# Input projection by block products: sums taken from blocks in SBUF, six direct tiles, gates in pieces

## The chip, the cores and the metric

The kernel runs on one core of a Trainium2 chip. The metric is the device time of one execution in microseconds, the median of several runs. The engines are named as the profile names them: PE (TensorE matmul), DVE (VectorE), ACT (ScalarE), POOL (GpSimd) and SP (SyncE, which here only issues loads). POOL issues all stores to DRAM, besides a little arithmetic.

## What is computed

One encoder block over 2048 tokens of width 1024, in float32. Only its first step is touched here: a norm of the input and one combined projection of width 3080, whose columns feed two attentions, a set of forget gates and two sets of values.

```python
h = rmsnorm(x, norm1_g[l])
proj = jnp.einsum('bsd,de->bse', h, w_in[l])
dq, dk, dv, fq, fk, fv, fg = jnp.split(proj, SPLITS, axis=-1)
...
log_f = jax.nn.log_sigmoid((fg + b_f[l]).astype(f32))
cum = jnp.cumsum(log_f, axis=1).transpose(0, 2, 1)
...
x = x + jnp.einsum('bse,ed->bsd', mix, w_out[l])
h2 = rmsnorm(x, norm2_g[l])
...
x = x + jnp.einsum('bsf,fd->bsd', jax.nn.silu(g) * u, w_down[l])
return rmsnorm(x, normf_g)
```

## The kernel before, in words

**Products.** A float32 operand is split into a high part (a cast on ACT, L159) and a low part (a subtraction on DVE, L160), and a product is three matmuls of 128x128 by 128x512: high by high, high by low, low by high. The tokens go in four chunks c of 512 (half 0 is c = 0 and 1, half 1 is c = 2 and 3), the 1024 inputs in two halves kh. So a half has four blocks b11 = (kh 0, first chunk), b21 = (kh 1, first chunk), b12 and b22 (the same of the second chunk), each stored by quarters q of 256 tokens. A pair of weight tiles against a half would be eight block products; the kernel makes seven (P1 to P7, in the order P1, P2, P6, P5, P7, P3, P4) out of sums of blocks of the tokens (P5 = b12 - b11, P7 = b22 - b12, P6 = b22 - P5, P4 = b21 - P6) and sums of blocks of the weights. P1, P2 and P3 take b11, b21 and b22 as they are.

**Stages.** `load_x`, `norm` or `norm_two` and `turn` (transposes on PE into PSUM, L240; gains applied by ACT and DVE, L246 and L248) make a block and store it to DRAM in `hop_d`. At the start the first four weight tiles go *without* sums (`e_major`, L327 to L329, 24 matmuls of 512 columns a chunk), against chunk 0, whose blocks are the operands P1 and P2, and then against chunk 1, whose blocks stand in the places of P4 and P3. During the second of these passes `quarter` loads the stored blocks of half 0 again, in pieces of two of the eight slices, makes the four sums on DVE (L273 to L279), splits P5, P7 and P6 into operands, and stores P4 (`tp_d`). Then a list of steps runs: `Features` (two weight tiles, seven products of 12 matmuls, L429 to L431) for six pairs of tiles, `Values` of half 0 and half 1 (28 steps each), and eight more `Features` for half 1. Ahead of each step stand loads (`advance_loads`), sums of weights (`advance_sums`, L403) and splits (`advance_splits`, 4 steps ahead, 3 in the values). Behind each step `take` copies a sum out of PSUM (L439, on ACT) or adds to it (L441, L444, L447, on DVE). Product P6 is summed into the PSUM bank of P1, and P7 into that of P6, so PE waits for the copy in between. `give` splits the result and stores it through one of three buffers `hl`.

**The background.** From the third step on, one call a step drives a generator `second_half`: load, norm and turn the blocks of chunks 2 and 3, load them again and sum them by `quarter`, then `value_sums` (four times: load the value weights from `w_t`, four sums on DVE, L534 to L541, four stores). What is left of it is run out behind the last of these steps, with `gates(0)`: 32 matmuls (L676 to L679), a copy, a small DMA from partitions 8 to 15 to partitions 0 to 7, sigmoid, log and a scan over time on DVE (L693).

**Order.** The code's own order sets each engine's queue, within which a scheduler may move instructions a little. Buffers are few: `hx` 6 tiles (x rows, blocks, loaded blocks, gates), `rawP` 4 (weights as loaded), `opP` 6 (split weights), `hlP` 3. A load whose buffer is still read waits at the head of SP's queue, and holds what stands behind it.

Of the kernel before, what the change touches and what calls it, by code (L numbers as in the profile page):

```python
# [19 lines left out]
P = 128  # L20
# [39 lines left out]
def block_kernel(  # L60
# [101 lines left out]
    with ExitStack() as c1:  # L162
# [37 lines left out]
        def load_x(t):  # L200
            xt = hxt([P, D], "xt")
            nc.sync.dma_start(out=xt, in_=x[t * P:(t + 1) * P, :])
            return xt

        def norm(xt):
# [3 lines left out]
            for h in range(2):  # L209
                nc.scalar.activation(bank(), xt[:, h * 512:(h + 1) * 512], AF.Square, accum_out=s2[:, h:h + 1])  # L210
            nc.gpsimd.tensor_tensor(ss, s2[:, 0:1], s2[:, 1:2], ALU.add)
            rstd_of(r, ss, 1)
            nc.scalar.activation(xt, xt, AF.Copy, scale=r)

        def norm_two(rows):

            rs = []
            for xt in rows:
# [3 lines left out]
                nc.scalar.activation(bank(), xt[:, 0:512], AF.Square, accum_out=s2[:, 0:1])  # L222
                b = xt[:, 512:1024]
                nc.vector.tensor_tensor_reduce(ut("sq"), b, b, 1.0, 0.0, ALU.mult, ALU.add, s2[:, 1:2])
# [3 lines left out]
            for xt, r in zip(rows, rs):  # L228
                nc.scalar.activation(xt[:, 0:512], xt[:, 0:512], AF.Copy, scale=r)
                nc.vector.tensor_scalar(xt[:, 512:1024], xt[:, 512:1024], r, None, ALU.mult)  # L230

        def turn(c, q, kh, rows, p=None):

            b = hxt([P, 4, 256], "hb")
            for k0 in range(0, 4, 2):
                ps = bank()
                for ki in range(2):
                    for i in range(2):
                        k = kh * 4 + k0 + ki
                        nc.tensor.transpose(ps[:, (2 * ki + i) * P:(2 * ki + i + 1) * P],  # L240
                                            rows[i][:, k * P:(k + 1) * P], ident)
# [12 lines left out]
        def quarter(half, q, k0, early):  # L254

            cs, ks_ = slice(q * 256, (q + 1) * 256), slice(k0, k0 + 2)

            def put(p, src):
                if early and p != "P4":
                    hi, lo = ops_p[p]  # L260
                    split(hi[:, ks_, cs], lo[:, ks_, cs], src)
                else:
                    nc.gpsimd.dma_start(out=tp_d[p][half, k0 // 2, q], in_=src)

            b = {}
            for c in range(2):
                r = hxt([P, 2, 2, 256], "hr")
                for kh in range(2):
# [1464 lines left out]
```

## Time and profile before

| | |
|---|---|
| median of 3 runs | 2878.27 us (2871.42 to 2880.87) |
| the profiled execution, whole | 2875.7 us |
| its span, first to last instruction | 2873.9 us |
| input projection, until PE's last matmul of it | 582.1 us |
| PE busy, and its part of the span | 2757.9 us, 96% |
| DVE, ACT, POOL busy | 1915.9, 1501.2, 635.9 us |
| moved by DMA | 470.77 MB, mean 164 GB/s |

A matmul is pipelined: its row lasts about 0.39 us, and a new one begins every 0.23 us, so PE counts as busy through a row of matmuls and a gap in it is idle time. "PEclk" is the clock granted to PE as a share of 2.4 GHz; at 0.50 it is 1.2 GHz. What ended a gap stands behind an arrow. In the page's 40 slices of the span the first four, to 287 us, show PE at 7 to 8 tenths and the DMA engines at 6 to 8; later PE is at 9 nearly everywhere.

### The profile page before, as it was taken

What the parts mean: (1) busy time and instruction counts of PE and PEld (TensorE: products, weight loads), DVE (VectorE), ACT (ScalarE), POOL (GpSimd) and SP (SyncE); (2) the same over time, 40 slices, a digit from 0 to 9 for tenths busy, and PEclk for the clock granted to TensorE, in tenths of its full rate; (3) what the DMA queues carried; (4) which work ended last, traced back from release to release, by engine and by line L of the source; (5) the groups of instructions that cost most, each with busy time, mean ns of one, the idle gap of its engine ahead of it and who ended that gap; (6) DMA issues with size and microseconds to landing.
All of it is one profiled execution on the core that took longest, in us unless ns stands there. A gap on an engine that the chain in (4) does not pass through costs nothing.

```text
span 2873.9 us, 40778 instructions
## 1 busy us (share of the span) xinstructions
PE 2757.9 (96%) x13938; PEld 2284.1 (79%) x13938; DVE 1915.9 (67%) x3818; ACT 1501.2 (52%) x3004; POOL 635.9 (22%) x1141
## 2 busy tenths in 40 slices
PE   7788999999999999998999999999999999999997
PEld 6666777879999978787877778778888788888886
DVE  6656556678888898887343766665676666665555
ACT  5633544467877878887333433333554433333444
POOL 3343012434344433333111111111000110110001
PEclk9999999999999999999999999999999999999999
DMA  8688644574334223432555544445766333334654
GB/s 289 234 274 272 246 166 159 159 214 142 89 102 122 76 77 102 109 84 81 199 203 185 200 161 155 137 151 191 244 233 225 122 100 102 110 110 145 217 202 161
DMA packets 183760, 470.77 MB, mean 164 GB/s; under 512 B 27968, under 2 KB 44496, under 8 KB 183552
## 3 DMA queue, kind: packets, MB, share of 16 engines
q1 hardware_dynamic: 135264, 324.88, 35.8%
q0 software_dynamic: 48256, 143.28, 14.1%
q8 instruction: 109, 1.79, 0.3%
q14 instruction: 99, 0.81, 0.1%
q10 hardware_dynamic: 32, 0.01, 0.0%
HBM read 316.38 MB, written 151.58 MB: 163 GB/s over the span
## 4 chain that ended last, share of the span: by engine, by line
PE 67%; issue 14%; DMA 4%; POOL 4%; ACT 3%; DVE 2%; SPq 0%; POOLq 0%; DVEq 0%; ACTq 0%
PE ps L1022 6%; PE psF L1359 6%; PE psF L1360 5%; PE psF L1361 5%; PE psF L1479 4%; PE psF L1478 4%; PE psF L1477 4%; PE psS L865 4%; PE psS L866 4%; PE psO L957 3%; PE psO L951 2%; PE psO L950 2%; ACT p_sb L895 2%; PE psF L429 2%; PE psF L430 2%
## 5 line engine op out<-in xcount | busy, mean ns | idle before, releaser
L1359 PE MATMUL psF<-hhP,wop 128*128 128x512 f32 x1232 | 479.2, 394 | 14.1 <-DVE u L1371 8.4
L1360 PE MATMUL psF<-hlP,wop 128*128 128x512 f32 x1232 | 482.0, 391 | 0.0
L1361 PE MATMUL psF<-hhP,wop 128*128 128x512 f32 x1232 | 480.8, 391 | 0.0
L895 ACT ACTIVATE p_sb<-p_sb,mx 128x1024 f32<-128x1024 f32 (+7 forms) x384 | 343.6, 901 | 25.4 <-DVE mx L876 17.5
L1359 PEld LDWEIGHTS psF<-hhP,wop 128*128 128x128 f32 x1232 | 232.3, 189 | 80.3 <-DVE u L1371 19.1
L865 PE MATMUL psS<-ks,q 128*128 128x512 f32 (+2 forms) x640 | 271.3, 424 | 3.6 <-DVE mx L882 2.7
L1361 PEld LDWEIGHTS psF<-hhP,wop 128*128 128x128 f32 x1232 | 232.3, 189 | 49.3 <-issue 0.2
L1360 PEld LDWEIGHTS psF<-hlP,wop 128*128 128x128 f32 x1232 | 232.5, 189 | 45.1
L159 ACT CAST wop<-sP 128x512 fp32r<-128x512 f32 x232 | 143.9, 621 | 235.8 <-PE psF L1361 188.8
L1022 PE MATMUL ps<-ident,p_sb 128*128 128x128 f32 x1632 | 252.2, 275 | 11.6 <-ACT thd L1048 7.5
L1477 PE MATMUL psF<-dop 128*128 128x512 f32 x616 | 239.6, 389 | 0.0
L1478 PE MATMUL psF<-dop 128*128 128x512 f32 x616 | 239.6, 389 | 0.0
L1479 PE MATMUL psF<-dop 128*128 128x512 f32 x616 | 239.6, 389 | 0.0
L866 PE MATMUL psS<-ks,q 128*128 128x512 f32 (+2 forms) x640 | 232.9, 365 | 0.0
L1022 PEld LDWEIGHTS ps<-ident,p_sb 128*128 128x128 f32 x1632 | 195.6, 141 | 43.0 <-ACT thd L1048 9.7
L160 DVE TENSOR_TENSOR wop<-sP,wop 128x512 fp32r<-128x512 f32 x232 | 159.2, 687 | 101.5 <-ACT wop L159 101.0
L159 ACT CAST dop<-wr 128x512 fp32r<-128x512 f32 x154 | 95.8, 622 | 202.9 <-PE psF L1479 187.9
L160 DVE TENSOR_TENSOR dop<-wr,dop 128x512 fp32r<-128x512 f32 x154 | 106.1, 689 | 134.2 <-ACT dop L159 133.9
L1369 ACT COPY u<-psF 128x512 f32<-128x512 f32 x132 | 77.5, 587 | 199.7 <-PE psF L1361 196.9
L429 PE MATMUL psF<-phP,wop 128*128 128x512 f32 x392 | 158.0, 407 | 19.9 <-ACT u L439 12.7
L142 DVE TENSOR_TENSOR th<-ps,th 128x512 fp32r<-128x512 f32 (+1 forms) x232 | 146.9, 650 | 32.5 <-ACT th L141 31.6
L1401 POOL DMA_DIRECT2D a_d<-u x88 | 47.6, 541 | 532.1 <-DVE u L1392 529.4
(257 smaller groups left out, 6434.8 us busy)
## 6 DMA issues: line engine op xcount, KB each, us to landing
ar<-a_d SPq DMA_DIRECT2D x70, 512.0 KB
wr<-in_w_gate_dram SPq DMA_DIRECT2D x44, 512.0 KB, 4.7
wr<-in_w_up_dram SPq DMA_DIRECT2D x44, 512.0 KB, 5.7
a_d<-u POOLq DMA_DIRECT2D x88, 256.0 KB, 3.3
wr<-wd_d SPq DMA_DIRECT2D x40, 512.0 KB, 4.2
we<-in_w_e_dram SPq DMA_DIRECT2D x36, 512.0 KB, 4.6
a_d<-t POOLq DMA_DIRECT2D x66, 256.0 KB, 2.8
q<-fq_d SPq DMA_DIRECT2D x64, 256.0 KB, 4.0
```

The lines of the kernel that those rows point to most:

```text
L159: nc.scalar.copy(hi, src)
L160: nc.vector.tensor_sub(lo, src, f32(hi))
L865: nc.tensor.matmul(pm[:, 0:mw], q[:, m, 0, qc], ks[:, m, cols], start=True, stop=False)
L866: nc.tensor.matmul(pm[:, 0:mw], q[:, m, 1, qc], ks[:, m, cols], start=False, stop=not last)
L895: nc.scalar.activation(pv, pv, AF.Exp, scale=-1.0, bias=st[m], accum_out=acc)
L1022: nc.tensor.transpose(ps[:, (2 * i + s) * P:(2 * i + s + 1) * P], p_of(u, s, m, k0 + i), ident)
L1359: nc.tensor.matmul(acc, o[:, 0, ks_], hh[:, k, :], start=first and k == 0, stop=False, **go)
L1360: nc.tensor.matmul(acc, o[:, 0, ks_], hl[:, k, :], start=False, stop=False, **go)
L1361: nc.tensor.matmul(acc, o[:, 1, ks_], hh[:, k, :], start=False, stop=k == 3, **go)
L1477: nc.tensor.matmul(acc, a[:, 0, bs], w[:, 0, :], start=first and m == 0, stop=False, **go)
L1478: nc.tensor.matmul(acc, a[:, 0, bs], w[:, 1, :], start=False, stop=False, **go)
L1479: nc.tensor.matmul(acc, a[:, 1, bs], w[:, 0, :], start=False, stop=m == NF // 2 - 1, **go)
```

## The change

Six tiles instead of four go without sums against chunks 0 and 1 (`N_DIRECT`), and the list of `Features` of half 0 has five pairs instead of six. `turn` hands back the block it made, which stays in SBUF: for half 0 the blocks of chunk 1 are kept and only those of chunk 0 are loaded again (`load_b`), for half 1 nothing is loaded again. Chunk 1's blocks, and b12 of chunk 3, are not stored any more. `block_sums` takes the place of `quarter`, with whole blocks, in three pieces. The rows of tokens 512 to 767 are loaded into buffers of the sums at once, the other two sets behind them. `norm` scales in two halves. `Features.split("P4")` comes together with P2. `value_sums` sums in place and runs on a generator of its own, every other step from the second on, beside `second_half`, which begins two steps sooner. `gates` writes to one tile, its one DMA and its scan come two steps apart, and they run beside the steps that follow. Splits are 4 steps ahead throughout; the operands of half 1 are asked for at the first step of a product instead of the third, and are split one step later.

```diff
-        tp_d = {p: dram.tile([2, 2, 2, P, 2, 256], F32, name=f"tp_d{p}") for p in ("P5", "P6", "P7", "P4")}
+        tp_d = {p: dram.tile([2, 2, P, 4, 256], F32, name=f"tp_d{p}") for p in ("P5", "P6", "P7", "P4")}
+        N_DIRECT = 6
...
-            nc.scalar.activation(xt, xt, AF.Copy, scale=r)
+            for h in range(2):
+                nc.scalar.activation(xt[h], xt[h], AF.Copy, scale=r)
...
-            nc.gpsimd.dma_start(out=hop_d[c, kh, q], in_=b)
+            if c == 0 or c == 2 or (c, kh) == (3, 1):
+                nc.gpsimd.dma_start(out=hop_d[c, kh, q], in_=b)
...
+            return b
...
-                    nc.sync.dma_start(out=r[:, kh], in_=hop_d[half * 2 + c, kh, q][:, ks_])
-                    b[kh, c] = r[:, kh]
-            b11, b21, b12, b22 = b[0, 0], b[1, 0], b[0, 1], b[1, 1]
-            yield
             nc.vector.tensor_sub(b11, b12, b11)
             nc.vector.tensor_sub(b12, b22, b12)
             put("P5", b11)
+            yield
             put("P7", b12)
+            nc.vector.tensor_sub(b22, b22, b11)
             yield
-            nc.vector.tensor_sub(b22, b22, b11)
             nc.vector.tensor_sub(b21, b21, b22)
             put("P6", b22)
             put("P4", b21)
             yield
...
+            put("P5", a22, a21, a22, ALU.add)
+            put("P7", a21, a11, a21, ALU.subtract)
             yield
...
+            put("P6", a11, a22, a11, ALU.subtract)
+            put("P3", a12, a12, a11, ALU.subtract)
             yield
...
-        first = [Features(0, e) for e in (4, 6, 10, 12, 14, 8)]
+        first = [Features(0, e) for e in (6, 10, 12, 14, 8)]
...
-                s[1].split(*s[2:])
+                if s[0] == "val":
+                    s[1].split(*s[2:])
+                elif s[2] != "P4":
+                    s[1].split(s[2])
+                    if s[2] == "P2":
+                        s[1].split("P4")
...
+            if e in (0, 2):
+                q = e // 2
+                pieces = block_sums(0, q, *b0, *hb[q])
+            next(pieces, None)
+            if e % 2:
+                next(pieces, None)
+            if e == 1:
+                b0 = load_b(0, 1)
...
-                g, g2 = ut("g"), ut("g2")
-                nc.scalar.copy(g[0:16, :], ps[0:16, :])
-                nc.sync.dma_start(out=g2[0:8, :], in_=g[8:16, :])
-                nc.vector.tensor_add(z[0:8, j, :], g[0:8, :], g2[0:8, :])
+                nc.scalar.copy(z[0:16, j, :], ps[0:16, :])
+                yield
+            g = hxt([P, 2, 512], "gl")
+            nc.sync.dma_start(out=g[0:8], in_=z[8:16])
+            yield
+            yield
+            nc.vector.tensor_add(z[0:8], z[0:8], g[0:8])
...
-            advance_splits(at + (3 if val else 4))
+            advance_splits(at + 4)
             s[1].multiply(*s[2:])
+            if gate:
+                next(gate, None)
...
-                    elif at > 2:
-                        next(bg, None)
+                    if at > 0:
+                        next(bg[0], None)
+                    if at % 2:
+                        next(bg[1], None)
...
-                if v.half == 0 and s[3] == 2:
+                if v.half == 0 and s[3] == 0:
                     waiting.append(load_op(1, s[2]))
-                if s[3] == 0 and (v.half == 0 and m or v.half == 1 and m == 0):
+                if s[3] == 1 and (v.half == 0 and m or v.half == 1 and m == 0):
```

Three places in the queues. First PE, at the turn of the last rows of chunk 1 (16 transposes), before, where `phP_148` is the operand P4 that holds chunk 1's first block:

```order
L329 MATMUL psF<-phP_138,wop 128x512
L240 MATMUL psF<-ident,xt 128x128 x16
L327 MATMUL psF<-phP_148,wop 128x512 x3
L328 MATMUL psF<-plP_149,wop 128x512
L329 MATMUL psF<-phP_148,wop 128x512
```

and now, where `phP_136` is the operand P1, chunk 0's:

```order
L334 MATMUL psF<-phP_138,wop 128x512
L246 MATMUL psF<-ident,xt 128x128 x16
L332 MATMUL psF<-phP_136,wop 128x512
L333 MATMUL psF<-plP_137,wop 128x512
L334 MATMUL psF<-phP_136,wop 128x512
```

Between the turn and the first product with the block that it makes there now stand the 24 matmuls of the sixth tile against chunk 0. Second, SP's queue while half 1's blocks are made, from a late set of rows (`xt`) on, before (`hr<-hp_d` loads blocks again, `wv<-in_w_t` loads value weights, for sums at L530):

```order
L202 DMA xt<-in_x_dram 128x1024 x2
L269 DMA hr<-hp_d 128x512 x8
L306 DMA we<-in_w_e_dram 128x1024 x2
L530 DMA wv<-in_w_t_dram 128x512 x2
L269 DMA hr<-hp_d 128x512 x6
L369 DMA cossin<-in_rope_dram 128x1x512 x2
```

and now, around the last set of rows (L535 is the old L530; L477 loads value weights for products):

```order
L311 DMA we<-in_w_e_dram 128x1024 x2
L535 DMA wv<-in_w_t_dram 128x512 x3
L209 DMA xt<-in_x_dram 128x1024 x2
L535 DMA wv<-in_w_t_dram 128x512
L477 DMA wv<-in_w_t_dram 128x2x512 x4
L374 DMA cossin<-in_rope_dram 128x1x512 x2
```

The loads of blocks are gone, and the loads for the value sums stand between those of the weights and those of x. Third, POOL's queue around the first norm of chunk 2 (`ss`, `rstd`), before:

```order
L356 DMA fq_d_86<-hl 256x1x256 x2
L211 TENSOR_TENSOR ss<-s_1004 128x1
L137 TENSOR_SCALAR rstd<-ss 128x1
L138 TENSOR_TENSOR rstd<-rstd,mhalf 128x1
L211 TENSOR_TENSOR ss<-s_1040 128x1
```

and now:

```order
L340 DMA fk_d_89<-hl 128x512
L542 DMA wv_d<-wv 128x512
L218 TENSOR_TENSOR ss<-s_1097 128x1
L542 DMA wv_d<-wv 128x512
L137 TENSOR_SCALAR rstd<-ss 128x1
L218 TENSOR_TENSOR ss<-s_1134 128x1
L138 TENSOR_TENSOR rstd<-rstd,mhalf 128x1
```

The norm's three small instructions now stand among the stores of the first value sums, which wait for DVE.

## Rows read from the trace of the kernel before

**Rows 1.** Busy time by stage: us, busy of PE, PEld, DVE, ACT, POOL, PEclk, DMA share, GB/s.
```profile
0.00:45.00 45.00, 32.15 (x188) 29.18 (x189) 29.68 (x65) 30.16 (x59) 19.44 (x43) 1.00 0.78 278
45.00:300.00 255.00, 210.19 (x875) 164.74 (x874) 162.67 (x260) 116.38 (x213) 90.72 (x162) 0.90 0.79 270
300.00:582.00 282.00, 278.88 (x1221) 224.30 (x1220) 164.02 (x242) 122.59 (x201) 68.17 (x119) 1.00 0.54 177
```

**Rows 2.** Waits of PE from 45 to 300 us: in total, times, the longest.
```profile
PE psF L429 <- ACT u L439: 10.9, 2, 7.2
PE psF L240 <- ACT xt L213: 10.6, 5, 4.9
PE psF L431 <- DVE wop L160: 6.4, 1, 6.4
PE psF L489 <- DVE wop L160: 6.1, 2, 4.1
PE psF L429 <- DVE u L441: 5.2, 2, 4.1
PE psF L327 <- ACT phP L159: 4.9, 1, 4.9
PE psF L429 <- ACT wop L159: 0.6, 1, 0.6
```

**Rows 3.** Busy time in the eight stretches at half clock before 300 us.
```profile
279.64:283.05 3.41, 3.41 (x10) 2.64 (x9) 2.29 (x4) 2.42 (x5) 0.00 (x0) 0.50 1.01 390
...
sum 51.20, PE 34.90 PEld 27.32 DVE 32.51 ACT 21.01 POOL 13.40; mean PE 4.36 PEld 3.41 DVE 4.06 ACT 2.63 POOL 1.68
```

**Rows 4.** Busy time in a full stretch, and the two with most DMA.
```profile
150.00:175.00 25.00, 23.66 (x103) 18.70 (x101) 17.14 (x29) 11.30 (x24) 16.87 (x31) 1.00 0.92 313
275.00:300.00 25.00, 18.91 (x68) 14.68 (x68) 17.38 (x26) 12.09 (x20) 2.70 (x5) 0.86 0.95 351
300.00:350.00 50.00, 50.00 (x222) 41.20 (x221) 30.21 (x40) 26.07 (x40) 6.47 (x12) 1.00 0.70 245
```

**Rows 5.** Timeline at 53 us: start, length, what [idle before, what ended it].
```profile
52.07 1.99 ACT L159 CAST phP<-hb 128x1024 fp32r<-128x1024 f32 x2 [2.90 <-DVE hb L246]
53.17 1.22 PE L327 MATMUL psF<-phP,wop 128*128 128x512 f32 x2 [4.86 <-ACT phP L159]
```

**Rows 6.** Timeline of DVE before PE's wait that ends at 86.1 us.
```profile
76.00 0.69 DVE L273 TENSOR_TENSOR hr<-hr 128x512 f32<-128x512 f32 x1 [1.53 <-DMA hr<-hp_d]
85.36 0.68 DVE L160 TENSOR_TENSOR wop<-we,wop 128x512 fp32r<-128x512 f32 x1
```

**Rows 7.** Timeline of a norm and the turn behind it, 132 to 142 us.
```profile
132.09 0.60 ACT L210 ACTIVATE psF<-xt 128x512 f32<-128x512 f32 x1 [3.35 <-DMA xt<-in_x_dram]
139.34 1.01 POOL L138 TENSOR_TENSOR rstd<-rstd,mhalf 128x1 f32<-128x1 f32 x1
141.59 1.75 PE L240 MATMUL psF<-ident,xt 128*128 128x128 f32 x7 [4.94 <-ACT xt L213]
```

**Rows 8.** Timeline of SP and DVE before PE's wait that ends at 207.2 us.
```profile
197.39 2.25 SPq L269 DMA_DIRECT2D hr<-hp_d  x2
203.47 0.69 DVE L274 TENSOR_TENSOR hr<-hr 128x512 f32<-128x512 f32 x1 [8.01 <-DMA tp_dP<-hr]
```

**Rows 9.** Timeline of SP and ACT before PE's waits at 236 and 242 us.
```profile
204.79 21.56 SPq L530 DMA_DIRECT2D wv<-in_w_t_dram  x6
234.29 1.14 ACT L159 CAST wop<-wv 128x512 fp32r<-128x512 f32 x2 [7.77 <-DMA wv<-in_w_t_dram]
```

**Rows 10.** Timeline of DVE and ACT before PE's waits at 279 and 293 us.
```profile
273.16 2.28 DVE L693 TENSOR_TENSOR_SCAN ge<-gone,gz 8x1024 f32<-8x1024 f32 x1
291.19 0.62 ACT L159 CAST fvo<-uv 128x512 fp32r<-128x512 f32 x1 [4.40 <-DMA fv_d<-fvo]
```

**Rows 11.** DMA issues from 0 to 300 us: count, KB each, median us to landing.
```profile
xt<-in_x_dram SPq DMA_DIRECT2D x16, 512.0 KB, 5.7
...
tp_dP<-hr POOLq DMA_DIRECT2D x20, 256.0 KB, 5.1
...
hr<-tp_dP SPq DMA_DIRECT2D x16, 256.0 KB, 6.9
```

More of the change, by code (lines that the diff above doesn't have):

```diff
@@ L198, in hlt, with load_x @@
             return hlp.tile(shape, dt, name=name, tag="hl")
-        def load_x(t):
+        def load_x(t, parts=False):
+            if parts:
+                xt = [sumP.tile([P, 512], F32, name="xh", tag="s") for _ in range(2)]
+                for h in range(2):
+                    nc.sync.dma_start(out=xt[h], in_=x[t * P:(t + 1) * P, h * 512:(h + 1) * 512])
+                return xt
             xt = hxt([P, D], "xt")
             nc.sync.dma_start(out=xt, in_=x[t * P:(t + 1) * P, :])
-            return xt
+            return [xt[:, 0:512], xt[:, 512:1024]]
         def norm(xt):
@@ L282, in quarter, with load_b @@
             yield
+        def load_b(c, q):
+            r = [hxt([P, 4, 256], "hr") for _ in range(2)]
+            for kh in range(2):
+                nc.sync.dma_start(out=r[kh], in_=hop_d[c, kh, q])
+            return r
         def load_op(half, p):
@@ L288, in load_op @@
                 if p in tp_d:
-                    for k in range(2):
-                        nc.sync.dma_start(out=r[q][:, 2 * k:2 * k + 2], in_=tp_d[p][half, k, q])
+                    nc.sync.dma_start(out=r[q], in_=tp_d[p][half, q])
                 else:
@@ L709, in second_half @@
             yield
-            ahead = []
+            yield
+            b = []
             for n, (c, q) in enumerate(todo_):
-                rows, nxt = nxt, None
+                rows = nxt
                 for r in rows:
@@ L715, in second_half @@
                     yield
+                yield
                 for kh in range(2):
-                    turn(c, q, kh, rows)
+                    b.append(turn(c, q, kh, rows))
                     yield
@@ L720, in second_half, with all_sums @@
                     nxt = load(n + 1)
-                for a in ahead:
-                    yield from a
-                ahead = []
                 if c == 3:
-                    ahead = [quarter(1, q, k0, False) for k0 in (0, 2)]
-            for a in ahead:
-                yield from a
+                    yield from block_sums(1, q, *b)
+                    b = []
+        def all_sums():
             for k in range(4):
                 yield from value_sums(k)
-        bg = second_half()
+        bg = [second_half(), all_sums()]
         waiting = []
+        gate = None
         for at, s in enumerate(steps):
@@ L745, in block_kernel @@
                         put_op(*waiting.pop(0))
-                    elif at > 2:
-                        next(bg, None)
+                    if at > 0:
+                        next(bg[0], None)
+                    if at % 2:
+                        next(bg[1], None)
                     if at == n_first - 1:
-                        for _ in bg:
-                            pass
-                        gates(0)
+                        for g in bg:
+                            for _ in g:
+                                pass
+                        gate = gates(0)
+                        next(gate)
+                        next(gate)
             else:
@@ L756, in block_kernel @@
                 v, m = s[1], ORDER.index(s[2])
-                if v.half == 0 and s[3] == 2:
+                if v.half == 0 and s[3] == 0:
                     waiting.append(load_op(1, s[2]))
-                if s[3] == 0 and (v.half == 0 and m or v.half == 1 and m == 0):
+                if s[3] == 1 and (v.half == 0 and m or v.half == 1 and m == 0):
                     put_op(*waiting.pop(0))
                 if v.half == 1 and s[2] == "P4" and s[3] == 3:
-                    gates(1)
+                    gate = gates(1)
+                    next(gate)
+                    next(gate)
+        for _ in gate:
+            pass
     with ExitStack() as c2:
```

86 lines of the change are left out of this document (38 added, 48 removed).

## The prediction

> **What bounds the kernel now.** I read the busy time by stage first. From 300 us on PE is full (278.9 of 282 us) at full clock; from 45 to 300 us it is busy 210.2 of 255 us, at a mean clock of 0.90 [rows 1]. From the last `Features` on, the instructions of all queues stand as they did, so all that the change can give lies before 582 us, and nearly all of it between 45 and 300. I read PE's waits there next: seven groups, together 10.9 + 10.6 + 6.4 + 6.1 + 5.2 + 4.9 + 0.6 = 44.7 us [rows 2]. Then the clock: behind the waits it stands at 0.50 (1.2 GHz) in eight stretches, in which PE works 34.9 us [rows 3]; at full clock that is half, so they cost 17.4 us. What can be won is 44.7 + 17.4 = 62.1 us, 2.2% of the execution. No engine but PE is full in this stage (DVE 162.7, ACT 116.4, POOL 90.7 of 255 us); the DMA engines are the nearest, at 0.79 and 270 GB/s [rows 1]. So PE waits not for work that is too much but for work that comes late in a queue, and the question is which of these waits the new order removes and which it makes.
>
> **The waits that go.** *The turn of the passes, 4.9.* PE's first product with chunk 1 stands right behind the transposes that make its last quarter, and waits for eviction and cast [rows 5]. Now 24 matmuls of the sixth tile stand between. A matmul costs 50 / 222 = 0.225 us in a full stretch [rows 4], so the cover is 5.4 us against a wait of 4.9. It just holds; were the cover gone, the 4.9 would be back.
>
> *The start of the features, 6.4 + 0.6 and one of 1.1 behind it.* DVE has the last quarter's sums and splits in its queue, which waited for a loaded block at 76.0, and comes to the weights' split at 85.4 [rows 6]. The new pass has six tiles, 6 x 24 x 0.225 = 32 us instead of 22, for the same sums, and half of the blocks need no load. I take all of it.
>
> *The norms of chunks 2 and 3, 10.6 in five waits.* ACT stands 3.4 us for rows of x, POOL's power comes late, and PE waits 4.9 [rows 2, 7]. The change puts one more step (12 x 0.225 = 2.7 us) between norm and turn. What is left of it, I put into the next part.
>
> *Half 1's blocks, 7.2.* DVE stands 8.0 us in a sum whose operand SP asked for at 197.4, 2.3 us of issuing and a landing before it [rows 8]; ACT's copy of P6 waits behind it. The arrow names a store, but that instruction reads only loaded blocks. Now the blocks are in SBUF and the load is gone. All of it.
>
> *The end of the features, 3.7 + 4.1.* SP spends 21.6 us on six loads for value sums, because their buffers are taken, and the first value weights behind them keep ACT 7.8 us [rows 9]. Now these sums come in earlier steps and the first value weights are asked for while features run. All of it.
>
> *The first values, 6.1 in two waits.* The gates' scan, 2.3 us, stands before splits on DVE, and a store of `fvo` keeps ACT 4.4 us [rows 10]. The scan moves on by steps and splits are one step (2.7 us) further ahead. The store stays slow, so between 2.0 (the first wait alone) and 6.1 go; I take 6.1, since the second wait, 4.1, has 2.7 us more cover and its casts come in front of the last `fvo`.
>
> With the waits goes the half clock behind them.
>
> **What is added.** *Matmuls.* Two more tiles without sums are 2 x 2 x 24 = 96 matmuls, a pair by products is 7 x 12 = 84: 12 more, 12 x 0.225 = 2.7 us on PE. DVE loses four sums and three additions and gains one split, ACT three copies for one cast; both have room, so that counts nothing.
>
> *The first turns.* ACT's queue now has two Squares of the next rows ahead of the cast of P2's second quarter; 2 x 0.60 = 1.2 us [rows 7]. If it hides, 0; if the whole chain of the norm comes in front, a wait like the longest for a norm, 4.9 [rows 2]. I take 1.2, since PE has another tile's matmuls to do.
>
> *The feature stretch.* Here the change adds waits. SP waits for P4's second half to be stored before it may load it: 5.1 + 6.9 = 12.0 us from the last sum [rows 11], and behind it stand x of chunk 2 and the first value weights; ACT's cast of P4 stands ahead of the copy of P1 that PE needs for P6. POOL has four stores of value sums around the first norm's instructions, and they wait for DVE, which waits for the value weights. A weight buffer comes free only when a value sum's store has landed. I don't price each one, since they share one resource, and bound the stretch by its transfers. From the first rows of chunk 2 to the last product of the features it moves, in units of 512 KB: x 8, value weights for sums 8, weights 6, first value weights 6, rotation tables 2, P4 1; stored 22 of results, 6 of blocks, 8 of sums, 8 of value sums; 75 in all, 39.3 MB. PE's work in it is 5 x 84 x 0.225 = 94.5 us and 64 transposes at 0.125 (1.75 / 7 at half clock [rows 7], halved), 102.5 us. At the fastest 25 us of the trace, 351 GB/s, the transfers take 112 us, at the next, 313, they take 126, at the stage's mean of 270 they take 146 [rows 1, 4]. I take the mean of the two fast ones, 332: 118 us, 16 over PE's work, since the stretch holds more bytes in a microsecond of PE's work (0.38 MB) than either of the two carried. The bounds are 0 (stores trail into the values, where the share falls) and 43.
>
> The Trainium skill has a rule that speaks against the change here: "DMA: Bandwidth & Descriptors", section Specifications, gives about 358 GB/s as a core's part of the memory's bandwidth. By it the 39.3 MB would take 110 us, an estimate, and the forecast would be about 9 us lower than by my 332. The trace agrees over 25 us, where 351 is the most, and not over 3.4 us, where 390 GB/s went through [rows 3].
>
> *The rest.* Gates beside the values, operands of half 1 asked for earlier, norms in two halves: POOL, ACT and DVE do the same work in smaller pieces while PE is full, so they count nothing. Without that cover it would be the scan, 2.3 us [rows 10].
>
> **The sum.** The profiled execution took 2875.7 us, 2.6 below the median of the runs. 2875.7 - 44.7 - 17.4 + 2.7 + 1.2 + 16 = 2833.5; with 2.6 for the median, 2836.
>
> **The rivals.**
> *A, the transfers set the pace.* The stretch gets no faster a rate than the stage's mean, and costs 43 instead of 16: 2836 + 27 = 2863. For it speaks that 50 us at 0.9 of the DMA engines are already there [rows 4]; against it, that less is moved than before (no blocks loaded again for half 1).
> *B, nothing new waits.* Stores trail, the norms are in time: 2836 - 16 - 1.2 = 2819. For it: value weights are asked for four steps, 10.8 us, ahead of their sums, and x's landing takes 5.7 [rows 11]. Against: the rows of chunk 3 are still normed in the call that loads them.
> *C, slower.* Each of the eight background loads (four sets of x, four of value weights) stops ACT or DVE in its queue until it lands, as the load did that ends at 203.5 [rows 8], and PE loses 7.2 us with it and an eighth of today's clock loss, 2.2. That is 8 x 9.4 = 75 in place of 16: 2836 + 59 = 2895. It decides from (62.1 - 3.9) / 8 = 7.3 us a load on; up to there the change still wins. For it: SP's queue has these loads in front of x. Against it: the two sets of chunk 2 and all value weights are asked for two to four steps (5.4 to 10.8 us) ahead of use.
> *D, no change.* The waits move and keep their sum, because PE was only waiting for the slowest queue in another place: 2870 to 2887.
>
> **How the numbers follow.** Forecast 0.50, with 2824 to 2852 as its own range (the stretch between 4 and 32); A 0.22, B 0.12, C 0.08, D 0.08. The range takes the forecast, B and most of A: 2819 to 2868. A measurement of this kernel tells 0.3%, 8.6 us, from no change. Faster by more than that: 0.50 + 0.22 + 0.12 less a little of A's upper end, 0.83; within it 0.09; slower 0.08.
>
> **What would show it.** Right: no wait of PE behind the last transposes of chunk 1; no wait for DVE's splits at the first feature; PE's last matmul of the projection at about 540 us instead of 582; waits of PE in the stage of 10 to 20 us in all, nearly all for norms and for the copy of P1; DMA share of the feature stretch near 0.9. A shows as that share with waits of PE spread over all products; B as a stage without waits above 2 us; C as waits of ACT and DVE for x and value weights of 7 us and more, eight times. Wrong would be the whole reading if the stage's waits go and the end does not come sooner, or if attention or the feed-forward part, which have the same instructions, changed by more than some us.

## The result and the profile after

| | before | changed |
|---|---|---|
| median of 4 runs | 2877.07 us (2871.42 to 2880.87) | 2841.62 us (2838.60 to 2842.74) |
| span of the profiled execution | 2873.9 us | 2840.9 us |
| PE's last matmul of the projection begins | 582.1 us | 549.5 us |

The ratio is 0.9877, 95% interval 0.9858 to 0.9895: 1.2% faster. The forecast was 2836, with 2819 to 2868 as its range, so it was 5.6 us too low. The end of the projection, forecast at about 540 us, came at 549.5. All of the gain lies in the projection: it ends 32.6 us sooner, the span is 33.0 us shorter. What comes behind has the same instructions and took 2291.8 and 2291.4 us.

The busy time by stage of the changed kernel, with the columns of [rows 1]:

```profile
0.00:45.00 45.00, 29.88 (x181) 26.70 (x182) 29.36 (x65) 29.75 (x59) 18.41 (x41) 0.96 0.75 271
45.00:300.00 255.00, 241.58 (x1057) 193.91 (x1055) 179.69 (x261) 135.22 (x240) 87.22 (x154) 0.96 0.80 273
300.00:550.00 250.00, 245.66 (x1060) 196.10 (x1058) 141.17 (x211) 104.78 (x175) 64.71 (x113) 0.99 0.51 164
```

From 45 to 300 us PE is now busy for 241.6 us where it was for 210.2 [rows 1]: 13.4 us idle instead of 44.8. PE's waits in that stretch, against the seven groups of [rows 2]:

```profile
PE psF L434 <- ACT u L444: 9.6, 3, 4.0
PE psF L246 <- ACT xt L221: 3.7, 3, 1.9
```

Of the old groups only the transposes' wait for a norm is still there, with 3.7 us for 10.6. There is none at the turn of the passes, at the first feature, at the sum of half 1's blocks, at the end of the features or at the first values. What is left beside it are three waits of P6 for ACT's copy of P1. The clock did not follow. The stretches of the stage at half clock, with PE's busy time in each, to be held against [rows 3]:

```profile
110.12:113.53 3.41, 3.41 (x10) 0.50 0.91 353
130.60:134.01 3.41, 3.41 (x10) 0.50 0.87 283
157.90:161.31 3.41, 3.21 (x8) 0.50 0.60 183
164.73:168.14 3.41, 3.33 (x14) 0.50 1.01 334
181.80:188.63 6.83, 5.32 (x13) 0.50 0.78 229
sum 20.47, PE 18.68; mean PE 3.74
```

PE still works 18.7 us at 1.2 GHz, where it worked 34.9. Waits fell to 30%, the half clock to 54%.

The three waits for the copy end at 129.5 (3.04), 158.1 (2.55) and 183.3 us (4.03), and each has another cause. Here is the first, on ACT: the norm's two scalings stand in the queue ahead of the copy (L444) and wait for POOL's power.

```profile
125.58 0.60 ACT L159 CAST hl<-u 128x512 fp32r<-128x512 f32 x1
127.64 1.33 ACT L221 ACTIVATE xt<-xt,rstd 128x512 f32<-128x512 f32 x2 [1.45 <-POOL rstd L138]
128.87 0.56 ACT L444 COPY u<-psF 128x512 f32<-128x512 f32 x1
```

The second, on POOL and DVE: P6 of half 1 is summed in place, over block b22, and so waits until the store of that block (L256) has landed, 8.8 us after its issue. Behind the sum stands the addition for the feature's result, and ACT's cast of that result stands ahead of the copy.

```profile
145.67 0.59 POOL L256 DMA_DIRECT2D hp_d<-hb  x1
154.48 1.23 DVE L277 TENSOR_TENSOR hb<-hb 128x1024 f32<-128x1024 f32 x1 [3.49 <-DMA hp_d<-hb]
```

The third, on SP and ACT: the last rows of x are asked for at 171.4, and ACT's squares wait 5.98 us for them with the copy behind. On SP they stand right behind three loads of value weights (L535), and the first of these has waited 7.8 us for the store of a value sum to land and free its buffer (the first line, from SP's waits between 90 and 240 us: in total, times, the longest). So the value sums beside the features make this wait; e8 bears it out.

```profile
SPq L535 <- DMA wv_d<-wv: 11.0, 2, 7.8
169.93 1.46 SPq L535 DMA_DIRECT2D wv<-in_w_t_dram  x3
171.43 1.00 SPq L209 DMA_DIRECT2D xt<-in_x_dram  x2
179.47 0.60 ACT L217 ACTIVATE psF<-xt 128x512 f32<-128x512 f32 x1 [5.98 <-DMA xt<-in_x_dram]
```

### The profile page after: what moved, and what is told of

The parts are those of the page before. It is cut to its first block, busy times and chain, and to the rows that moved or that the text cites. A ratio compares the mean times of both kernels' runs of the same rounds, so it can differ in the third digit from the quotient of the medians.

```text
span 2840.9 us, 40678 instructions
## 1 busy us (share of the span) xinstructions
PE 2753.1 (97%) x13950; PEld 2282.7 (80%) x13950; DVE 1910.0 (67%) x3788; ACT 1502.0 (53%) x3004; POOL 629.8 (22%) x1125
## 3 DMA queue, kind: packets, MB, share of 16 engines
q0 software_dynamic: 47232, 140.14, 13.8%
## 4 chain that ended last, share of the span: by engine, by line
PE 67%; issue 18%; POOL 4%; DMA 4%; ACT 4%; DVE 3%; SPq 0%; POOLq 0%; DVEq 0%; ACTq 0%
PE ps L1056 6%; PE psF L1393 6%; PE psF L1394 6%; PE psF L1395 6%; PE psF L1513 4%; PE psF L1512 4%; PE psF L1511 4%; PE psS L899 4%; PE psS L900 4%; PE psO L991 3%; PE psO L985 2%; PE psO L984 2%; PE psF L434 2%; PE psF L436 2%; PE psF L435 2%
## 5 line engine op out<-in xcount | busy, mean ns | idle before, releaser
L1393 PE MATMUL psF<-hhP,wop 128*128 128x512 f32 x1232 | 478.4, 394 | 13.4 <-DVE u L1405 10.9
L1394 PEld LDWEIGHTS psF<-hlP,wop 128*128 128x128 f32 x1232 | 231.8, 188 | 44.8
L434 PE MATMUL psF<-phP,wop 128*128 128x512 f32 x364 | 147.3, 409 | 13.5 <-ACT u L444 10.5
```

The lines of the kernel that those rows point to most:

```text
L1393: nc.tensor.matmul(acc, o[:, 0, ks_], hh[:, k, :], start=first and k == 0, stop=False, **go)
L1394: nc.tensor.matmul(acc, o[:, 0, ks_], hl[:, k, :], start=False, stop=False, **go)
```

## The experiments

Two theories of what makes the time of the feature stretch. **Queues**: each new wait comes from an instruction that stands in the wrong place of one queue, and bytes don't matter. **Transfers**: the stretch lasts as long as its 39 MB take, as the prediction had it for its term of 16 us. Beside them the question whether half clock follows the waits.

All times in one table. The ratio is to executions of the kernel before that were taken beside the kernel in its row, so it can order two rows otherwise than the medians. "End" is the start of PE's last matmul of the projection, "idle" is 255 us less PE's busy time from 45 to 300, "half" is PE's busy time there at half clock, each from one profile. What follows the projection has the same instructions in all of them and took from 2282.7 to 2294.7 us in the profiles, so the end tells an edit apart better than the time does.

One profile says less about "half" than about the rest, since the half clock varies without any edit. Behind the projection the same instructions work from 15.8 to 33.3 us at half clock in the fourteen profiles (idle 51.9 to 59.8 us). At 17 to 21 us, before any of the edits e1 to e12 takes hold, it is 3.0 to 3.4 us in four of the thirteen changed kernels and nothing in nine. So I also give the mean granted clock of whole executions where a fall of "half" is read as a gain: it was 0.986 to 0.989 in the four of the changed kernel, and 0.001 of it stands for 5.7 us at half clock.

| kernel | median, us | ratio to before, 95% interval | end | idle | half |
|---|---|---|---|---|---|
| before | 2877.1 | 1 | 582.1 | 44.8 | 34.9 |
| changed | 2841.6 | 0.9877 (0.9858 to 0.9895) | 549.5 | 13.4 | 18.7 |
| e1 norm in two steps | 2834.7 | 0.9859 (0.9843 to 0.9876) | 543.8 | 13.1 | 6.6 |
| e2 more steps | 2842.2 | 0.9881 (0.9861 to 0.9901) | 546.8 | 16.3 | 11.1 |
| e3 P2 twice | 2832.0 | 0.9850 (0.9833 to 0.9868) | 543.2 | 7.3 | 3.4 |
| e4 more bytes, early | 2841.5 | 0.9878 (0.9857 to 0.9900) | 550.2 | 17.8 | 15.3 |
| e5 more bytes, in the features | 2844.5 | 0.9884 (0.9853 to 0.9916) | 553.4 | 23.4 | 14.0 |
| e6 mended | 2836.7 | 0.9861 (0.9833 to 0.9889) | 542.3 | 13.7 | 6.8 |
| e7 four tiles without sums | 2849.5 | 0.9908 (0.9884 to 0.9932) | 553.5 | 20.7 | 18.5 |
| e8 value sums late | 2841.5 | 0.9877 (0.9852 to 0.9902) | 555.9 | 23.5 | 13.8 |
| e9 P1 ahead | 2840.8 | 0.9887 (0.9866 to 0.9908) | 544.9 | 13.4 | 14.7 |
| e10 all mends | 2832.3 | 0.9854 (0.9834 to 0.9873) | 534.2 | 10.4 | 8.7 |
| e11 blocks loaded again | 2850.4 | 0.9916 (0.9895 to 0.9936) | 565.7 | 29.1 | 22.4 |
| e12 gates at once | 2839.0 | 0.9877 (0.9860 to 0.9893) | 545.3 | 13.9 | 12.5 |

### Do the transfers set the pace? (e4, e5)

```diff
+                    if at % 2 == 0:
+                        nc.gpsimd.dma_start(out=more_d[at // 2], in_=f32(ops_p["P1"][0][:, 0:2, :]))
```

> At every second step of the first five features POOL stores another 512 KB, a piece of operand P1, to a scratch tensor: 18 stores, 9.4 MB more in the stretch. Transfer theory, as the prediction had it: 9.4 MB at 332 GB/s, 28 us more. Queue theory: 18 issues of 0.55 us on POOL and landings somewhat longer, 0 to 8 us more.

This run missed its place. The scheduler issued the 18 stores as soon as their operand was there, from 27.8 to 66.1 us, ahead of the features, so the run says nothing on the features. It shows something else. The row of 45 to 93.5 us, the passes without sums:

```profile
45.00:93.50 48.50, 48.50 (x224) 40.39 (x223) 37.81 (x50) 23.89 (x38) 15.47 (x26) 1.00 0.98 377
```

For 48.5 us 377 GB/s went through, at a DMA share of 0.98, and PE waited for nothing. In e5 the same stores are held in their places on POOL's queue (`tc.keep_in_program_order`); they go out from 95.6 us on.

> As the run with more bytes, but the 18 extra stores of 512 KB are held in their places on POOL's queue, so that they go out during the first five features (there they had all gone out between 28 and 66 us, before the features). Transfer theory, as the prediction had it: 9.4 MB at 332 GB/s, 28 us more. Queue theory: 18 issues of 0.6 us on POOL, landings longer by some us, so that two or three waits of 2 to 5 us grow or come: 2 to 12 us more.

The time rose by 2.9 us and the end of the projection by 3.9, not by 28. From the first to the last product of the features, the changed kernel first, then e5:

```profile
93.45:221.64 128.19, 114.77 (x490) 91.60 (x489) 80.47 (x129) 63.82 (x133) 55.91 (x100) 0.92 0.83 281
```

```profile
93.00:228.90 135.90, 112.48 (x490) 89.96 (x489) 80.95 (x129) 64.20 (x133) 63.35 (x117) 0.91 0.91 321
```

The stretch grew by 7.7 us and moved 321 GB/s in place of 281. So in the changed kernel the transfers had room left, and they do not set its pace. Seventeen of the 18 stores fall into it. Bytes do cost something: idle time rose from 13.4 to 23.4 us, one wait of 8.9 us for a norm among it, in whose chain ACT stands 5.9 and 2.7 us for rows of x. Transfer theory falls in the form in which the prediction used it.

### The waits one by one (e1, e2, e6)

```diff
-                for r in rows:
-                    norm(r)
-                    yield
+                r0 = squares(rows[0])
+                yield
+                scale(rows[0], r0)
+                r1 = squares(rows[1])
+                yield
+                scale(rows[1], r1)
                 yield
```

> In the background of the features a norm is written in two steps: its squares in one, its scaling in the next one, behind the copies of the step between. Queue theory: the wait of 3.0 us at 129.5 us (PE for ACT's copy of P1, which stands behind a scaling that waits 1.45 us for POOL's power and takes 1.3 us itself) goes, and its stretch of half clock with it, 1.7 us; the other two waits for that copy have other causes and stay. Projection ends at 545 to 547 us instead of 549.9, the time falls by 3 to 5 us; the transposes may wait 1 to 2 us more, since scaling comes later. Transfer theory (the stretch lasts as long as its 39 MB): the wait shows up elsewhere, the end stays within 1 us.

The wait of 3.0 us is gone. ACT in e1, at the place that answers to 127 us above (L447 is the copy): no scaling stands between.

```profile
127.08 0.58 ACT L221 ACTIVATE psF<-xt 128x512 f32<-128x512 f32 x1
127.61 0.19 ACT L221 ACTIVATION_READ_ACCUMULATOR psF<-xt 128x1 f32 x1
127.70 0.56 ACT L447 COPY u<-psF 128x512 f32<-128x512 f32 x1
```

But the idle time as a whole is what it was, 13.1 for 13.4 us: the transposes, whose rows are now scaled a step later, wait 7.8 instead of 3.7. PE's waits in e1:

```profile
PE psF L249 <- ACT xt L214: 7.8, 5, 3.4
PE psF L437 <- ACT u L447: 3.5, 3, 2.4
PE psF L437 <- DVE u L449: 1.7, 2, 0.9
```

The projection ends 5.7 us sooner all the same, and in the stage that is the clock: half-clock work fell from 18.7 to 6.6 us, which is 6.0 us of time. The other executions bear it out: the mean granted clock was 0.990 to 0.993 in the four of e1, and each of them is shorter than each of the changed kernel's. That the clock follows from the edit is likely by this; why it does, with the same idle time, is not shown.

```diff
+                if c == 3:
+                    yield
+                    yield
                 for r in rows:
...
                 if c == 3:
+                    yield
                     yield from block_sums(1, q, *b)
```

> Two empty steps between the load of chunk 3's rows and their norm, one empty step between the last turn of a quarter and its sums, both times. Queue theory: the wait of 2.5 us at 158.1 us (DVE's sum in place stands 3.5 us for the store of the block it overwrites) and that of 4.0 us at 183.3 us (ACT's squares stand 6.0 us for rows of x) go, with 1.7 and 2.7 us of half clock: 11 us in all at most, 6 to 11 less time, projection ends at 539 to 544. The sums of the last quarter come five steps (13 us) later, which the first values may feel by up to 3 us. Transfer theory: no change beyond 1 us.

A miss. The squares no longer wait for x, but ACT's copy at 184.1 is as late as before, now behind a scaling. And the empty step ahead of the sums did not keep them apart from the turn. On POOL and DVE of e2:

```profile
200.63 0.59 POOL L270 DMA_DIRECT2D tp_dP<-hb  x1 [6.79 <-DVE hb L272]
203.44 0.55 POOL L256 DMA_DIRECT2D hp_d<-hb  x1 [2.22 <-DVE hb L252]
212.27 1.22 DVE L277 TENSOR_TENSOR hb<-hb 128x1024 f32<-128x1024 f32 x1 [6.72 <-DMA hp_d<-hb]
```

The scheduler had moved P5's sum (L272) in among the evictions of the turn, so the order in the code is not the order in the queue, and the sum over b22 (L277) stands close behind the block's last eviction (L252). POOL stands idle until that eviction and then issues the store of b22 (L256) at once; the store of P5 (L270) in front of it costs nothing there. The store lands 8.7 us after its issue, and the sum waits 6.7 of them; PE then waits 5.4 us at 214. So this wait is the landing itself, and the edit put no distance between the store and the sum.

e6 has e1's edit, holds P5's store behind the store of b22 (`tc.issue_after`), puts the squares of chunk 1's rows behind the casts of P2 at the start, and gives the gates two more steps before their scan.

> Four edits at once, each against one wait of the changed kernel: a norm's scaling one step behind its squares (as in the first experiment), the store of P5 behind the store of the block that the next sum overwrites (it stood in front, and DVE's sum waited 3.5 and 5.1 us for the late landing), the gates' scan two steps later in half 1, and at the start the squares of the next rows behind the casts of P2. Queue theory with the clock on the waits: PE's idle time between 45 and 300 us falls from 13.4 to 5 to 8 us, its half-clock work from 18.7 to under 7, the 3.0 us at 408 us go with their 2.9; the time falls to 2824 to 2831. If something shared is behind the waits: they move, and it stays at 2834 to 2842.

Queue theory expected 5 to 8 us of idle time, and 13.7 were measured. The long waits are gone but for one of 2.6 us, and ten of 0.4 to 1.9 stand in their place. The wait at 402 us stayed (3.1). And the new order of the stores did not shorten DVE's waits for the landing: 5.0 and 3.7 us in the two sums over b22, where the changed kernel has 3.5 and 5.1.

```profile
147.75 1.23 DVE L286 TENSOR_TENSOR hb<-hb 128x1024 f32<-128x1024 f32 x1 [4.99 <-DMA hp_d<-hb]
201.15 1.22 DVE L286 TENSOR_TENSOR hb<-hb 128x1024 f32<-128x1024 f32 x1 [3.73 <-DMA hp_d<-hb]
```

In the stage only the clock paid: 6.8 us of half-clock work (mean granted clock of the four executions 0.989 to 0.990). So the edits moved the waits, as the rival said, and yet the projection ended 7.2 us sooner.

### More cover (e3, e9, e10)

```diff
+            again = s[1].op.get("P2") if at in (8, 15, 22) else None
             s[1].multiply(*s[2:])
+            if again:
+                s[1].multiply("P2", again)
```

> In the three features in which PE waits for the copy of P1, the twelve matmuls of P2 are issued twice, the second time over the first: 36 matmuls more, 8.1 us of work, in front of those waits. If the half clock hangs on the waits: 9.6 us of waits and 6.0 us of clock go against 8.1 us of work, so the time falls by 4 to 7.5 us though PE does more. If half clock comes from something else in the stretch: between 1.5 us less and 0.5 more. If transfers set the pace: no change.

The second product goes into the same bank, over the first. With 36 matmuls more the projection ends 6.3 us sooner than in the changed kernel. By the medians the kernel is 9.6 us faster; in the profiles, too, some 6 us more come from behind the projection, where the instructions are the same. PE's waits in e3:

```profile
PE psF L246 <- ACT xt L221: 4.8, 4, 1.9
PE psF L434 <- ACT u L444: 1.7, 2, 1.1
PE psF L434 <- DVE u L446: 0.8, 1, 0.8
```

The waits for the copy fell from 9.6 to 1.7 us, half-clock work in the stage from 18.7 to 3.4. In the stage that is 6.1 us of waits and 7.7 of clock against 8.1 us of work: 5.7. The waits alone would not pay for the work; the clock does, and it stood higher in all four executions (0.991 to 0.992). It bears out that clock is lost with the waits and that filling them with work, even useless work, can give it back. e9 tries the same cover without work: the first product of a feature goes ahead of the last one of the feature before, so that 24 matmuls stand between P1 and P6.

```diff
+        for n in range(7, n_first, 7):
+            steps[n - 1], steps[n] = steps[n], steps[n - 1]
```

> In the first five features the P1 of a feature is issued ahead of the P4 of the one before, so that two products (24 matmuls, 5.4 us) instead of one stand between P1 and the P6 that needs its copy; no work is added. If those waits come from a cover that is too short, as the run with P2 twice suggests (waits of the stage 13.4 to 7.3 us): waits fall by 5 to 9 us, half-clock work by 8 to 14 (4 to 7 us of time), 2827 to 2833. If the gain there came from the longer stretch of PE's work, which gave all other queues 8 us more: the waits move to the transposes and the end, 2836 to 2842.

The waits for the copy halve, those for the norm more than double, and the idle time is 13.4 us again:

```profile
PE psF L246 <- ACT xt L221: 8.7, 3, 3.4
PE psF L434 <- ACT u L444: 4.8, 2, 4.2
```

So the cover of one product is not the cause by itself, and the time lies in the range of the second reading. What e3 gave and e9 does not are 8.1 us more of PE's work in the stretch, in which all queues get on. That this is the cause is argued, not shown. e10 joins e6 and e9, adds one step before the transposes, and holds the gates' last DVE instructions back.

> The mended kernel with P1 ahead as well, one empty step more between the last scaling and the transposes, and the gates' last DVE work held in its place in the queue. Cover theory: the waits at P6 and before the transposes are both gone but for 2 to 5 us, the 3.1 us at 402 us go, half-clock work in the stage under 4 us: 2820 to 2828. Against it: as in the mended kernel the waits that are removed come back at other places, 2832 to 2838.

```profile
PE psF L443 <- DVE u L455: 8.2, 4, 3.4
PE psF L443 <- ACT u L453: 1.9, 2, 1.2
PE psF L445 <- DVE wop L160: 0.2, 1, 0.2
```

The time lies in the range against cover theory, which had 2820 to 2828. Waits for norms are gone. What is left stands behind the sums in place on DVE and its splits. The wait at 408 us is gone too: PE idles 0.9 us from 300 us on, where the changed kernel idles 4.3. The projection ends at 534.2, 15.3 us sooner. By the medians the gain is 9.3 us, less than in the profiles (13.1). e3 and e10 are both faster than before. Each of their executions is shorter than each of the changed kernel's, though the intervals of the ratios overlap; between the two no difference can be told.

### Parts of the change undone (e7, e8, e11, e12)

```diff
-        N_DIRECT = 6
+        N_DIRECT = 4
...
-            if e in (2, 4):
-                q = e // 2 - 1
+            if e in (2, 3):
+                q = e - 2
...
-        first = [Features(0, e) for e in (6, 10, 12, 14, 8)]
+        first = [Features(0, e) for e in (4, 6, 10, 12, 14, 8)]
```

> Four tiles without sums instead of six, six features instead of five, the rest as changed. By the prediction's steps the waits at the turn of the passes (4.9) and at the start of the features (8.1) come back with their half clock (up to 8), less 12 matmuls (2.7): 10 to 18 us more than the changed kernel, 2852 to 2860. Rival: the kept blocks alone, and splits asked for earlier, remove those waits: 2839 to 2846.

7.9 us slower, between the two theories. The turn of the passes waits again, the start of the features does not: its first product (L434) follows the last direct one without a gap.

```profile
53.43 0.50 PE L332 MATMUL psF<-phP,wop 128*128 128x512 f32 x1 [3.80 <-ACT phP L159]
...
77.40 0.39 PE L334 MATMUL psF<-phP,wop 128*128 128x512 f32 x1
77.62 0.39 PE L434 MATMUL psF<-phP,wop 128*128 128x512 f32 x1
```

```diff
-                    if at % 2:
-                        next(bg[1], None)
```

> The value sums are not run beside the features any more but all behind the last of them. By the prediction's steps the waits at the end of the features come back (7.8 us and 5.1 us of half clock), while the waits behind POOL's value-sum stores (1.8 us at 108 us, 1.9 at 164, part of the 3.0 at 129) go: 4 to 11 us more than the changed kernel, 2846 to 2853. Rival: moving them into the features only moved the waits: 2838 to 2844.

A wait behind the features is there again, now at the first values, and longer than the two it stands for (7.8):

```profile
249.38 0.79 PE L493 MATMUL psF<-wop,phP 128*128 128x512 f32 x1 [13.36 <-ACT wop L159]
```

The features, though, took 118.9 us instead of 127.8, with 10.1 us idle. Without the value sums' loads in front of them, the rows of x keep ACT 1.7 us where they kept it 9.0 (ACT's waits from 95 to 222 us, the changed kernel first, then e8), and of PE's waits for the copy one of 1.6 us is left.

```profile
ACT psF L217 <- DMA xt<-in_x_dram: 9.0, 2, 6.0
```

```profile
ACT psF L217 <- DMA xt<-in_x_dram: 1.7, 1, 1.7
```

So the value sums beside the features cost them 8.9 us, 3.3 of it idle time and 5.4 half clock, and save a longer wait behind them: by the end of the projection the changed order wins 6.4 us. The time itself shows no difference (2841.5): what follows the projection took 2282.7 us in this profile, the least of all, with the least idle time of all there (51.9 us) and 20.1 us at half clock where the changed kernel has 33.3.

```diff
-            if c == 0 or c == 2 or (c, kh) == (3, 1):
+            if c != 1:
...
                 if c == 3:
+                    b = load_b(2, q) + load_b(3, q)
+                    yield
                     yield from block_sums(1, q, *b)
```

> The blocks of half 1 are stored and loaded again for their sums, a step before them, as in the kernel before; all else as changed. By the prediction's step the 7.2 us wait behind the sum that stands for a loaded block comes back, with 2 to 3 us of half clock, less the wait of 2.6 us for the in-place sum (the loaded copy has no store to wait for): 4 to 8 us more than the changed kernel, 2846 to 2850. Rival: one step and the landing of 6.9 us are covered by the spare steps: 2839 to 2844.

8.8 us slower, a little above what was expected; the projection ends 16.2 us later. DVE's first sum stands for the loaded blocks:

```profile
160.40 1.23 DVE L272 TENSOR_TENSOR hr<-hr 128x1024 f32<-128x1024 f32 x1 [9.97 <-DMA hr<-hp_d]
```

PE waits 7.84 us at 164.1 and 9.15 at 231.6 behind such sums.

```diff
                         gate = gates(0)
-                        next(gate)
-                        next(gate)
+                        for _ in gate:
+                            pass
...
                     gate = gates(1)
-                    next(gate)
-                    next(gate)
+                    for _ in gate:
+                        pass
```

> The gates of both halves are written in one go again, behind the last feature of half 0 and the last values of half 1, in place of pieces beside the steps that follow; splits stay four steps ahead. By the prediction's step the waits at the first values come back, the scan's 2.0 us and perhaps the 4.1 us, with up to 3.4 us of half clock: 2 to 8 us more than the changed kernel, 2844 to 2850. Rival: splits four steps ahead cover the scan, and in half 1 the wait of 3.0 us at 408 us, which the kernel before has not (1.0 and 1.4 us there), goes with its 2.9 us of half clock: 2836 to 2842.

Neither. No wait comes back at the first values, and the wait in half 1 stays:

```profile
405.34 0.80 PE L434 MATMUL psF<-phP,wop 128*128 128x512 f32 x1 [2.96 <-DVE u L446]
```

So the gates in pieces gain nothing here. Splits one step further ahead, or value weights that are there in time, are enough for the first values; which of the two was not tried. The wait in half 1 is made by DVE's gate instructions, in one go as in pieces, which stand in its queue for ACT: in e10, where the last of them are held back, it is gone.

## Why the prediction held, step by step

The sum, profile against profile, up to the end of the projection. Measured terms: idle time, plus half of PE's work at half clock, by stretch; the matmuls' term is what is left over, uncertain by 2 us, since the recorded clock stretches don't end where matmuls do. The sum misses by 9.6 us, more than the time does (5.6): the profiled executions do not lie at the medians.

| term | forecast, us | measured, us |
|---|---|---|
| waits of before | -44.7 | -44.7 |
| half clock of before | -17.4 | -17.4 |
| matmuls added | +2.7 | -1.3 |
| first turns (15 to 45 us) | +1.2 | +4.0 = 2.3 idle + 3.4 / 2 |
| feature stretch | +16 | +22.7 = 13.4 idle + 18.7 / 2 |
| rest, from 300 us on | 0 | +4.1 = 1.2 idle + 5.8 / 2 |
| sum | -42.2 | -32.6 |

**Right.** The waits to be won were 44.7 us, and all of them are gone but 3.7 of the 10.6 for norms, which the forecast had among the new ones. *Turn of the passes*: covered by the sixth tile; with four tiles 3.8 of the 4.9 us are back (e7). *Half 1's blocks*: loaded again they cost more than the 7.2 us (e11). *End of the features*: the sums' new place removes it (e8). That the new waits would be 10 to 20 us, for norms and for the copy of P1, was right to the place: 13.3 us, in those two groups alone. Rival C, background loads that stop ACT and DVE eight times, shows once in that size, 5.98 us for x at 179.5. Rival B, nothing new waits, did not come, and neither did D, no change.

**Right in size, wrong in cause.** *Start of the features*, 8.1 us: it was not the longer pass of six tiles, since with four it does not wait either (e7); what remains are the blocks that are kept and the splits asked for earlier, which were not told apart. *First values*, 6.1 us: not the scan's new place (e12).

**Wrong: "With the waits goes the half clock behind them."** Half clock came back with the new waits: 18.7 us of work in the stage, 3.4 at the start, 5.8 in half 1, together 27.9 / 2 = 13.9 us that the sum had at nothing of its own. Without it the sum would have missed by 4 us to the other side. The new waits are short, 0.9 to 4.0 us, and one of them took about as much clock as one of the longer ones before: 1.6 us (9.3 for six waits), where it was 1.2 (17.4 for fourteen). For one us of wait that is 0.39 us of clock before (17.4 / 44.7) and 0.70 now (9.3 / 13.4). How much clock a given wait takes is open, as the variation without an edit says.

**Wrong: the reason for the 16 us.** They were worked out from bytes at 332 GB/s. The changed stretch ran at 281 GB/s with a DMA share of 0.83, not "near 0.9", and 9.4 MB more made it 7.7 us longer, not 28 (e5). PE's work in it, the length less the idle time and half of the work at half clock, was 105.4 us for the 102.5 of the forecast. Of the single causes that the prediction named and did not price, one makes a long wait: a weight buffer that comes free only when a value sum's store has landed, with x behind it on SP (the third wait). Two it did not have: the sum in place that waits for a store to land, and the scaling ahead of the copy, behind POOL's power. That 16 came as near 22.7 as it did is luck. Rival A, which stood on the same ground, falls with it. The rule of the Trainium skill ("DMA: Bandwidth & Descriptors", section Specifications, about 358 GB/s as a core's part) did not bind either: 377 GB/s over 48.5 us in e4 are above it.

**Wrong, small: "they count nothing".** The gates of half 1 with the operands around them cost 4.1 us at 408 us, since a wait of 2.96 us stands there for ones of 1.0 and 1.4 us before, with half clock behind it. And the start: ACT's squares and scalings ahead of P2's casts cost 2.3 us instead of 1.2; the 1.7 us of half clock at 18 us came with gaps that the kernel before has as well, without half clock, and nine of the other changed kernels have none there either.

**What set the idle time?** In the changed kernel, e1, e6, e9 and e12 it is 13.1 to 13.9 us, while the single waits differ in place and owner. It fell only where PE got more work (e3, 7.3) or where all queues were put right at once (e10, 10.4). It rose with more bytes (e5, 23.4). So no single queue makes it; which chain of the background sets it stays open. One candidate: from 90 to 240 us loads on SP wait 64.0 us in all for stores of value sums to land. Without these, in e8, the features still have 10.1 us of idle time, 4.3 of it behind a sum in place, so it is at most a part.

## What to carry to other kernels

Price a wait with the clock behind it, and price the new waits the same way: where one wait becomes several short ones, the idle time falls and the half clock may stay. A wait that is taken away at one engine's queue can show up at the next one, as in e1, e6 and e9; look at the sum of PE's idle time, not at the wait that was mended. An instruction that writes in place over a block that is being stored waits for the landing, 8 to 9 us after the issue in the changed kernel. Putting that store in front of another did not help by itself (e6); a sum into a buffer of its own was not tried. When a load comes late, read what stands in front of it in its queue: the buffer that was not free may be another load's.

## What the runs showed of the hardware

**Half clock varies by more than the waits do.** With 13 to 14 us of idle time the half-clock work of the stage was 18.7, 14.7, 12.5, 6.8 and 6.6 us, so 3.3 to 9.4 us of time. Length alone doesn't decide. In the changed kernel the clock fell behind two gaps of 0.90 us with one transpose between them (first rows below). In e3 it stayed at 1.0 behind gaps of 1.06 and 0.90 at the same place (second), and in e1 through a gap of 2.40 (third). Nor do the instructions: the same ones behind the projection worked 15.8 to 33.3 us at half clock.

```profile
108.11 0.33 PE L246 MATMUL psF<-ident,xt 128*128 128x128 f32 x1 [0.90 <-ACT xt L221]
109.34 0.88 PE L246 MATMUL psF<-ident,xt 128*128 128x128 f32 x6 [0.90 <-ACT xt L221]
```

```profile
108.00 0.33 PE L246 MATMUL psF<-ident,xt 128*128 128x128 f32 x1 [1.06 <-ACT xt L221]
109.23 0.98 PE L246 MATMUL psF<-ident,xt 128*128 128x128 f32 x7 [0.90 <-ACT xt L221]
```

```profile
156.36 0.50 PE L437 MATMUL psF<-phP,wop 128*128 128x512 f32 x1 [2.40 <-ACT u L447]
```

**More work can be less time.** With 36 useless matmuls in front of three waits the projection ended 6.3 us sooner (e3), by 6.1 us less idle time and 7.7 us less lost to the clock, against 8.1 us of work.

**Transfers at 377 GB/s beside a full PE.** 48.5 us at a DMA share of 0.98, PE busy for 48.5 of them (e4); the fastest 25 us of the kernel before had 351 [rows 4].
